# The opening of a two-layer encoder trunk: gains transposed ahead of x, x's high part taken from PSUM tile by tile, first splits in a written order, bf16 filling products

## The chip, the cores and the metric

The kernel runs on one core of one Trainium2 chip. The metric is the device time of one execution in microseconds. A profiled execution also gives a trace; its span runs from the first to the last instruction and is a little shorter than the device time. In the lines of the profile, PE is TensorE's matrix product, PEld its load of the stationary operand, DVE VectorE, ACT ScalarE, POOL GpSimd, SP the engine that issues most transfers; "L367" is line 367 of the kernel.

## What is computed

Two layers over 256 tokens of width 1024, everything in float32. The change touches the start of the first layer only: the root-mean-square norm of x and the gate and up projections of the first feed-forward block.

```python
def rmsnorm(x, g):
    y = x32 * lax.rsqrt(jnp.mean(x32 * x32, axis=-1, keepdims=True) + EPS)
    return (y * g.astype(jnp.float32)).astype(x.dtype)

def swiglu(h, w_gate, w_up, w_down):
    return (jax.nn.silu(h @ w_gate) * (h @ w_up)) @ w_down

for i in range(DEPTH):
    x = x + 0.5 * swiglu(rmsnorm(x, ffn1_norm[i]), ffn1_w_gate[i], ffn1_w_up[i], ffn1_w_down[i])
    h = rmsnorm(x, mix_norm[i])
    ...                                  # self attention and memory attention on h, projections
    x = x + jnp.concatenate([o_s, o_m], axis=-1) @ w_out[i]
    x = x + 0.5 * swiglu(rmsnorm(x, ffn2_norm[i]), ffn2_w_gate[i], ffn2_w_up[i], ffn2_w_down[i])
```

The widths: x is (256, 1024), w_gate and w_up are (1024, 2816), w_down (2816, 1024).

## The kernel before

**Products of float32 by two parts.** Each float32 operand is split into a high part of the type fp32r, which TensorE takes in one pass, and a low part, the difference. A product is then three matmuls into one PSUM bank (`dense`): high by high (line 542), high by the weight's low part (545), low of x by the weight's high part (548). Weights are split after they have landed: ScalarE copies the raw block to the high part (`split_hi`, line 367), VectorE subtracts (`split_lo`, line 385).

**The feed-forward block.** The 2816 columns go in 11 groups of 256. A chunk of weights is 512 rows of one group, gate beside up, 128 x 2048 in SBUF, in four blocks `q` of 128 rows. Three raw buffers and four pairs of split buffers rotate. For each chunk both token tiles (`tb` 0 and 1, 128 tokens each) pass through the four blocks: 24 matmuls of 128 x 512. The first four chunks are (group 0, rows 0 to 511), (group 1, rows 0 to 511), (group 0, rows 512 to 1023), (group 1, rows 512 to 1023); of the first chunk, blocks 0 and 1 are taken for both token tiles, then blocks 2 and 3.

**The opening.** The first chunk's load comes in four pieces (gate and up for each block), the second's in two, every later one in one. The order of the issues is: the first feed-forward norm's gains (`g1row`, on ScalarE's queue), the first half of x for token tile 0, block 0's gate (SP) and up (ScalarE's queue), the first half of x for tile 1, the rest of the first chunk, the second chunk, the second halves of x, the third chunk. TensorE meanwhile multiplies the identity by itself (`warm`, float32). x's halves (128 x 512) are prepared by `prep_half`: four transposes into a PSUM bank, one VectorE product with the gains into `y` (line 612), one ScalarE copy of `y` to the high part `xh` (650), one VectorE subtraction to the low part `xl` (654). The gains themselves are rows when they land: TensorE transposes them (`gps`, line 1762), VectorE copies them to `gcol` (1764). Three microseconds later on the planner's clock a ScalarE square of the half of x follows (`square`, line 667); the row norm's factor is applied only when a group's products leave PSUM (`evac`, line 728).

**What sets the order.** The program is a list of instructions per engine in the order in which Python emits them. That order comes from a model clock, `Flow`: `now` is TensorE's time, `free` holds the times at which ScalarE, VectorE and GpSimd become free; steps are generators that wake at a time or on a condition, and each emitted instruction moves the clock by an estimate (`flow.pe`, `flow.act`, `flow.dve`). `loader`, `split_hi` and `split_lo` are such generators and go by estimated arrivals (`c.block`, `c.arrive`, from `dma_free`). The hardware keeps each engine's order, and its semaphores keep the dependencies, whatever the estimates say. At the start the order is: five `warm` products, `now` set to 2.7, the gains' transpose at 3.9 with two more fillers and one at 5.6, and `prep_half` for the four halves of x at 3.4, 5.8, 12.6 and 13.4.

Of the kernel before, what the change touches and what calls it, by code (L numbers as in the profile page):

```python
# [12 lines left out]
F32 = mybir.dt.float32  # L13
# [3 lines left out]
AF = mybir.ActivationFunctionType  # L17
# [3 lines left out]
P = 128  # L21
# [20 lines left out]
T_TR = 0.107  # L42
SLACK = 0.4
AHEAD = 0


class Flow:
# [10 lines left out]
        (self.idle if idle else self.threads).append([self.now, gen])  # L58

    def pe(self, dur):  # L60
        self.now += dur
        return self.now + HOP

    def eng(self, e, dur):
# [103 lines left out]
def kernel(  # L168
# [34 lines left out]
    def bank(name, shape=(P, 4, P)):  # L203
        return banks.take(list(shape), F32, name)
# [67 lines left out]
    class Item:  # L272
# [3 lines left out]
        def __init__(self, raws, uses=8, w=1):  # L276
            self.raws, self.uses = raws, uses
            self.hi = self.lo = None
            self.hit, self.lot, self.st = [None] * 7, [None] * 7, [None] * 4
            self.n, self.frees, self.takes, self.gives, self.guest = 1, 1, 0, 0, False  # L280
            self.sums, self.t = [], []
            self.index = len(items)
            w = 1 if len(items) < 2 else w
            self.units = [(self.own(q, w), q, w, None) for q in range(0, 4, w)]
            items.append(self)

# [7 lines left out]
            return ts[q // 4][:, q % 4 * 512:(q % 4 + w) * 512]  # L294

    chunks, items = [], []
    raw_left = [NRAW]
    hl_left = [NHL]
    xt_room = [False]
# [12 lines left out]
    def loader():  # L312
        for i, c in enumerate(chunks):
            yield lambda: raw_left[0] > 0
            raw_left[0] -= 1
            c.raw = wraw.tile([P, 2048], F32, tag="raw", name=f"raw{i}")
            dma_free[0] = max(dma_free[0], flow.now)
            n = len(c.parts)
            lat = LAT + slow[0] if i > 1 else 0.6
            for j, (dst, src) in enumerate(c.parts):  # L320
                (nc.scalar if i == 0 and j == 1 else nc.sync).dma_start(out=dst(c.raw), in_=src)
                dma_free[0] += 3.0 / n
                if i < 2 and j % 2:
                    for q in range((j - 1) * 4 // n, (j + 1) * 4 // n):
                        c.block[q] = dma_free[0] + lat
                if i == 0 and j == 1:
                    table_hint(AF.Silu)
                    load_x(1, 0)
                    dma_free[0] += 0.75
            c.arrive = dma_free[0] + lat  # L330
            c.block = [t or c.arrive for t in c.block]
            if i == 1:
                for tb in range(2):
                    load_x(tb, 1)
                    dma_free[0] += 0.75
            if i > 4 and late_done[0] < len(late_loads):
                dst, src = late_loads[late_done[0]]
                late_done[0] += 1
                nc.sync.dma_start(out=dst, in_=src)
                dma_free[0] += 0.3  # L340
# [7 lines left out]
    def split_hi():  # L348
        for i, it in enumerate(items):
            yield lambda: (hl_left[0] >= it.n and all(r.raw is not None for r in it.raws)  # L350
                           and (xt_room[0] or not it.guest))
            hl_left[0] -= it.n
            if it.guest:
                xt_room[0] = False
            yield max(r.block[0] for r in it.raws)
            it.hi, it.lo = ([whl.tile([P, 2048], F32R, tag=x, name=f"{x}{i}_{j}") for j in range(it.n)]
                            for x in ("hi", "lo"))
            if it.guest:
                for x, ts in (("xh", it.hi), ("xl", it.lo)):
                    ts += [xtp.tile([P, KT, P], F32R, tag=f"{x}{j}", name=f"g{x}{j}") for j in range(2)]  # L360
            for src, q, w, dep in it.units:
                yield max(r.arrive if dep is not None else r.block[q + w - 1] for r in it.raws)
                if dep is not None:
                    yield lambda: it.st[dep] is not None
                    yield it.st[dep]
                yield calm_a(i)
                nc.scalar.copy(out=it.part(0, q, w), in_=src())  # L367
                t = flow.act(512 * w)
                it.hit[q:q + w] = [t] * w

    def split_lo():
        for i, it in enumerate(items):
            if it.sums:
                yield lambda: all(r.raw is not None for r in it.raws) and g2.left >= it.takes + 2
                yield max(r.arrive for r in it.raws)
                it.t += [g2.take([P, 512], F32, "wsum") for _ in range(it.takes)]
                for j, (x, y) in enumerate(it.sums):
                    yield calm_v(i)
                    nc.vector.tensor_sub(it.t[j], x(), y())  # L379
                    it.st[j] = flow.dve(512)  # L380
            for src, q, w, dep in it.units:
                yield lambda: it.hit[q] is not None
                yield it.hit[q]
                yield calm_v(i)
                nc.vector.tensor_sub(it.part(1, q, w), src(), it.part(0, q, w).bitcast(F32))  # L385
                t = flow.dve(512 * w)
                it.lot[q:q + w] = [t] * w
            raw_left[0] += it.frees
            g2.give(it.gives)
# [80 lines left out]

    def plan_ffn(l, nm, wg, wu, wd):
        def parts(g, c):
            pieces = (4, 2)[len(chunks)] if len(chunks) < 2 else 1
            a = cols4(wg[l], c, g * 256, 256, 0, pieces)
            b = cols4(wu[l], c, g * 256, 256, 256, pieces)
            return [q for ab in zip(a, b) for q in ab]

        gu = {}
        pair = PAIR[l, nm]
        work = [(g, c) for g in range(NG) for c in range(2)]  # L480
        if (l, nm) == (0, 1):
            work[:4] = [(g, c) for c in range(2) for g in range(2)]
        if pair is not None:
            rest = [w for w in work if w[0] not in (pair, pair + 1)]
            n = 2 * pair
            p = iter(rest[n:])
            work = rest[:n]
            loads = {}
            for x in ("11", "m1", "p", "12", "m5", "p", "22", "m7", "p", "m6", "p", "m3", "p", "p", "21", "m2", "p", "m4"):
                work.append(next(p) if x == "p" else x)  # L490
            work += list(p)
            blocks = {"11": (pair, 0), "12": (pair + 1, 0), "22": (pair + 1, 1), "21": (pair, 1)}
            raws = [Chunk(parts(*blocks[x])) for x in ("11", "12", "22", "21")]
            made, mk = pair_items(raws)
            which = dict(zip(("11", "12", "22", "21"), raws))
        for w in work:
            if w in ("11", "12", "22", "21"):
                chunks.append(which[w])
            elif isinstance(w, str):
                mk[w]()  # L500
            else:
                gu[w] = add_chunk(parts(*w), 8, 2)
        plan[l, nm, "gu"] = gu
        plan[l, nm, "work"] = [w for w in work if w not in ("11", "12", "22", "21")]
        if pair is not None:
            plan[l, nm, "pair"] = made
        dn = []
        for c in range(NG):
            dn.append(add_chunk(turned2(wd[l], c)))
            if c in SEVEN[l, nm]:  # L510
                seven_item(dn[-1], c != SEVEN[l, nm][0])
            elif c >= NG - 3:
                u = dn[-1].units
                u[1], u[2] = u[2], u[1]
        plan[l, nm, "dn"] = dn
# [1240 lines left out]
    flow.step()  # L1756
    xt = Xt(PAIR[0, 1] is not None)

    def start_gain():
        yield 3.9  # L1760
        tp = bank("gps0")
        nc.tensor.transpose(out=tp[:, 0, :16], in_=g1row, identity=ident[:16, :16])
        yield flow.pe(T_TR)
        nc.vector.tensor_copy(gcol[:, 0:16], tp[:, 0, :16])
        banks.give()
        flow.dve(16)
        first_gain.append(True)
        warm(2)
        yield 5.6
        warm(1)  # L1770

    def start(tb, hf, t):
        yield t
        yield from prep_half(xt, tb, hf, GC_FFN1, 3.0)

    def warm(n):
        for _ in range(n):
            nc.tensor.matmul(out=wb[:, 0, :], lhsT=ident, rhs=ident, start=True, stop=True)

    wb = bank("warm")  # L1780
    banks.give()
    warm(5)
    flow.now = 2.7
    flow.spawn(start_gain())
    for tb in range(2):
        for hf in range(2):
            flow.spawn(start(tb, hf, (3.4, 12.6, 5.8, 13.4)[2 * tb + hf]))
    flow.spawn(gain_columns())
    flow.spawn(rope_setup(), idle=True)
    flow.spawn(lambda_setup())  # L1790
# [59 lines left out]
```

## Time and profile before

| | us |
|---|---|
| median of 3 runs | 948.93 |
| lowest and highest | 948.30, 949.33 |
| the profiled execution | 948.83 |
| its span | 947.0 |
| first product with weights starts, from the span's start | 7.42 |
| first product of the second chunk starts | 15.06 |

The page also has the DMA's share. Slice by slice (40 slices of 23.7 us) it reads so:

```profile
DMA  9968799688525486896847679775632367589561
GB/s 296 284 212 250 228 325 329 231 268 254 178 90 164 121 258 210 266 291 225 259 143 217 214 233 290 236 252 173 203 130 76 131 219 225 188 260 329 183 217 47
```

A digit is the mean busy share of the 16 DMA engines in tenths. Records of matmuls overlap: one of 128 x 512 lasts 0.39 us in the trace while the next starts 0.23 us after it, so the pace is read from the distance of the starts. A row of the timeline joins equal instructions of one engine that follow each other ("x4"), with the start of the first and the time to the end of the last.

### The profile page before, as it was taken

Reading aid. Unit: us, or ns where it says so; the run is one execution under the profiler, and the core shown is the slowest. Engines: PE = TensorE matmul, PEld = TensorE weight load, DVE = VectorE, ACT = ScalarE, POOL = GpSimd, SP = SyncE. Lnnn points to the kernel's source line nnn. Section 1 sums busy time; section 2 is a strip of 40 time slices with the busy share of each in tenths; the row PEclk is TensorE's granted clock in tenths of the full one; section 3 lists DMA queues with packets and bytes.
Section 4 is the critical chain, followed back from the end, with each engine's and each line's share of the span. In section 5 each row is a group of like instructions: output and inputs, shape, how many; then the busy total and the mean of one; then the engine's idle time right before and its main releaser. Section 6 shows DMA issues by size and latency. Waiting matters only on the chain. (4 is left out here: it accounts for less than half of the span.)

```text
span 947.0 us, 13323 instructions
## 1 busy us (share of the span) xinstructions
PE 940.3 (99%) x4456; PEld 773.2 (82%) x4456; DVE 829.7 (88%) x1501; ACT 590.8 (62%) x1126; POOL 108.6 (11%) x160
## 2 busy tenths in 40 slices
PE   9999999999999999999999999999999999999998
PEld 7888888887878888888888888888887788888887
DVE  6989988888777889989889899796999899998995
ACT  6656666677786746647546656563777765655671
POOL 0000038731210000000000000000334100000000
PEclk9999999999999999999999999999999999999999
DMA  9968799688525486896847679775632367589561
GB/s 296 284 212 250 228 325 329 231 268 254 178 90 164 121 258 210 266 291 225 259 143 217 214 233 290 236 252 173 203 130 76 131 219 225 188 260 329 183 217 47
DMA packets 172574, 206.13 MB, mean 218 GB/s; under 512 B 10265, under 2 KB 147290, under 8 KB 172506
## 3 DMA queue, kind: packets, MB, share of 16 engines
q1 hardware_dynamic: 169498, 202.92, 67.0%
q10 hardware_dynamic: 3008, 2.37, 0.8%
q8 instruction: 35, 0.57, 0.2%
q14 instruction: 33, 0.27, 0.1%
HBM read 190.04 MB, written 15.20 MB: 217 GB/s over the span
## 5 line engine op out<-in xcount | busy, mean ns | idle before, releaser
L367 ACT CAST hi<-raw 128x512 fp32r<-128x512 f32 (+1 forms) x466 | 334.8, 770 | 152.4 <-DMA raw<-in_ffn_w_up_dram 45.7
L385 DVE TENSOR_TENSOR lo<-raw,hi 128x512 fp32r<-128x512 f32 (+1 forms) x466 | 392.2, 877 | 23.1 <-ACT hi L367 22.5
L548 PE MATMUL gu<-hi,xl 128*128 128x512 f32 x528 | 206.0, 390 | 0.0
L542 PE MATMUL gu<-hi,xh 128*128 128x512 f32 x528 | 206.0, 390 | 0.0
L545 PE MATMUL gu<-lo,xh 128*128 128x512 f32 x528 | 205.8, 390 | 0.0
L545 PEld LDWEIGHTS gu<-lo,xh 128*128 128x128 f32 x528 | 99.2, 188 | 21.0 <-DVE lo L385 0.4
L548 PEld LDWEIGHTS gu<-hi,xl 128*128 128x128 f32 x528 | 99.3, 188 | 21.0 <-DVE xl L654 0.4
L542 PEld LDWEIGHTS gu<-hi,xh 128*128 128x128 f32 x528 | 99.4, 188 | 20.4
L548 PE MATMUL acc<-hi,ht 128*128 128x512 f32 x270 | 105.6, 391 | 0.0
L542 PE MATMUL acc<-hi,ht 128*128 128x512 f32 x270 | 105.1, 389 | 0.0
L545 PE MATMUL acc<-lo,ht 128*128 128x512 f32 x270 | 105.1, 389 | 0.0
L367 ACT CAST hi<-wsum 128x512 fp32r<-128x512 f32 x83 | 49.0, 620 | 40.0 <-DVE wsum L379 37.0
L548 PE MATMUL pj<-hi,xl 128*128 128x512 f32 x160 | 63.9, 400 | 0.0
L545 PE MATMUL pj<-lo,xh 128*128 128x512 f32 x160 | 63.6, 397 | 0.0
L542 PE MATMUL pj<-hi,xh 128*128 128x512 f32 x160 | 63.5, 397 | 0.0
L545 PEld LDWEIGHTS acc<-lo,ht 128*128 128x128 f32 x270 | 50.7, 188 | 10.6
L542 PEld LDWEIGHTS acc<-hi,ht 128*128 128x128 f32 x270 | 50.7, 188 | 10.4
L548 PEld LDWEIGHTS acc<-hi,ht 128*128 128x128 f32 x270 | 50.7, 188 | 10.4
L585 POOL TENSOR_TENSOR xr<-v,nhalf 128x1 f32<-128x1 f32 x12 | 8.6, 719 | 429.6 <-DVE v L583 429.6
L385 DVE TENSOR_TENSOR lo<-wsum,hi 128x512 fp32r<-128x512 f32 x83 | 53.7, 676 | 0.0
L728 ACT ACTIVATE sil<-gu,xr 128x256 f32<-128x256 f32 x72 | 33.8, 469 | 24.7 <-PE gu L548 23.1
L585 POOL TENSOR_TENSOR hf<-v,nhalf 128x8 f32<-128x8 f32 (+1 forms) x20 | 32.1, 1607 | 83.2 <-DVE v L583 74.1
(244 smaller groups left out, 1531.5 us busy)
## 6 DMA issues: line engine op xcount, KB each, us to landing
raw<-in_ffn_w_down_dram SPq DMA_DIRECT2D x176, 256.0 KB, 4.4
raw<-in_ffn_w_gate_dram SPq DMA_DIRECT2D x82, 512.0 KB, 4.6
raw<-in_ffn_w_up_dram SPq DMA_DIRECT2D x82, 512.0 KB, 5.2
raw<-in_w_in_dram SPq DMA_DIRECT2D x32, 512.0 KB, 5.1
hd<-hb SPq DMA_DIRECT2D x44, 256.0 KB, 4.9
hr<-hd SPq DMA_DIRECT2D x44, 256.0 KB, 5.1
raw<-in_w_out_dram SPq DMA_DIRECT2D x8, 1024.0 KB, 4.9
raw<-in_w_mem_kv_dram SPq DMA_DIRECT2D x4, 1024.0 KB, 9.0
```

The source lines that it names most:

```text
L367: nc.scalar.copy(out=it.part(0, q, w), in_=src())
L385: nc.vector.tensor_sub(it.part(1, q, w), src(), it.part(0, q, w).bitcast(F32))
L542: nc.tensor.matmul(out=ps, lhsT=xh, rhs=wh, start=start, stop=False)
L545: nc.tensor.matmul(out=ps, lhsT=xh, rhs=wl, start=False, stop=False)
L548: nc.tensor.matmul(out=ps, lhsT=xl, rhs=wh, start=False, stop=stop)
L585: nc.gpsimd.tensor_tensor(out=dst, in0=v[:, :n], in1=nhalf[:, :n], op=ALU.pow)
L728: nc.scalar.activation(sil, ps[tb][:, 0:256], AF.Silu, scale=xt.r[tb])
```

## The change

It replaces the opening by a written order, and gives the planner other numbers for the first 7.5 us and the first three chunks.

- Filling products: bf16, 128 x 128, on a zeroed stretch of `junk` (a memset on VectorE), 23 at the start, two behind the gains' transpose and five behind the first four transposes of x, in place of five, two and one in float32 on the identity.
- The gains' transpose and its copy are emitted ahead of x's transposes.
- Token tile 0, first half: ScalarE takes the high part of each 128 x 128 tile from PSUM with the gain as its scale (`high`), with the weight blocks' high parts 0 and 1 in between; VectorE makes `y` from PSUM (`scaled`), then the low part of weight block 0, then x's low part.
- Token tile 1, first half: `y` as before, high part by one ScalarE copy of `y` behind block 2's high part; VectorE makes block 1's low part between `y` and the low part of x.
- The squares of x's first halves are set to 18.0 on the planner's clock. The second halves are started at 13.2 and 14.0.
- The third chunk is loaded in two pieces and split block by block. The first three chunks' arrivals are constants (`FIRST`).
- `Flow.pe` doubles each product's duration while `now` is under 7.5.

```diff
+COLD = 7.5
...
     def pe(self, dur):
-        self.now += dur
+        self.now += dur * (2 if self.now < COLD else 1)
...
-            w = 1 if len(items) < 2 else w
+            w = 1 if len(items) < 3 else w
...
+    FIRST = ((4.7, 6.1, 6.9, 8.6), (10.2, 10.2, 12.1, 12.1), (15.1, 15.1, 16.6, 16.6))
...
-                if i < 2 and j % 2:
+                if i < 3 and j % 2:
                     for q in range((j - 1) * 4 // n, (j + 1) * 4 // n):
-                        c.block[q] = dma_free[0] + lat
+                        c.block[q] = FIRST[i][q]
...
-            c.arrive = dma_free[0] + lat
+            c.arrive = dma_free[0] + lat if i > 2 else FIRST[i][3]
...
-            yield max(r.block[0] for r in it.raws)
+            if i:
+                yield max(r.block[0] for r in it.raws)
...
             for src, q, w, dep in it.units:
+                if i == 0 and q < 3:
+                    continue
...
             for src, q, w, dep in it.units:
+                if i == 0 and q < 2:
+                    continue
...
-            pieces = (4, 2)[len(chunks)] if len(chunks) < 2 else 1
+            pieces = (4, 2, 2)[len(chunks)] if len(chunks) < 3 else 1
...
-    def start_gain():
-        yield 3.9
-        tp = bank("gps0")
...
-        warm(2)
-        yield 5.6
-        warm(1)
-
-    def start(tb, hf, t):
-        yield t
-        yield from prep_half(xt, tb, hf, GC_FFN1, 3.0)
+    wz = junk[:, 0:P]
+    nc.vector.memset(wz, 0.0)
+    wb = bank("warm")
+    banks.give()
 
     def warm(n):
         for _ in range(n):
-            nc.tensor.matmul(out=wb[:, 0, :], lhsT=ident, rhs=ident, start=True, stop=True)
-
-    wb = bank("warm")
+            nc.tensor.matmul(out=wb[:, 0, :], lhsT=wz, rhs=wz, start=True, stop=True)
+
+    def turned(tb):
+        tp = bank("xtp")
+        return tp, [turn(tp[:, k, :], xs[tb][:, k * P:(k + 1) * P]) + 0.1 for k in range(4)]
+
+    def high(tb, tp, k):
+        nc.scalar.activation(xt.h[tb][:, k, :], tp[:, k, :], AF.Copy, scale=gcol[:, GC_FFN1 + k:GC_FFN1 + k + 1])
+        xt.th[tb][k] = flow.act(P)
+
+    def scaled(tb, tp):
+        y = xt.y[tb, 0] = g2.take([P, 4, P], F32, "y")
+        nc.vector.tensor_tensor(out=y, in0=tp, in1=gcol[:, GC_FFN1:GC_FFN1 + 4].unsqueeze(2).broadcast_to([P, 4, P]),
+                                op=ALU.mult)
+        banks.give()
+        return flow.dve(512)
+
+    def low(tb):
+        nc.vector.tensor_sub(xt.l[tb][:, 0:4, :], xt.y[tb, 0], xt.h[tb].bitcast(F32)[:, 0:4, :])
+        xt.t[tb][0:4] = [flow.dve(512)] * 4
+        flow.spawn(square(xt, tb, 0, 18.0))
+
+    def first_hi(q):
+        nc.scalar.copy(out=items[0].part(0, q), in_=items[0].own(q)())
+        items[0].hit[q] = flow.act(512)
+
+    def first_lo(q):
+        nc.vector.tensor_sub(items[0].part(1, q), items[0].own(q)(), items[0].part(0, q).bitcast(F32))
+        items[0].lot[q] = flow.dve(512)
+
+    def start(tb, t):
+        yield t
+        yield from prep_half(xt, tb, 1, GC_FFN1, 3.0)
+
+    warm(23)
+    tp = bank("gps0")
+    nc.tensor.transpose(out=tp[:, 0, :16], in_=g1row, identity=ident[:16, :16])
+    nc.vector.tensor_copy(gcol[:, 0:16], tp[:, 0, :16])
     banks.give()
+    warm(2)
+    first_gain.append(True)
+    flow.now = 4.0
+    tp, _ = turned(0)
     warm(5)
-    flow.now = 2.7
-    flow.spawn(start_gain())
-    for tb in range(2):
-        for hf in range(2):
-            flow.spawn(start(tb, hf, (3.4, 12.6, 5.8, 13.4)[2 * tb + hf]))
+    flow.free.update(A=4.3, V=4.95)
+    high(0, tp, 0)
+    flow.free["A"] = 4.7
+    first_hi(0)
+    for k in range(1, 4):
+        high(0, tp, k)
+    flow.free["A"] = 6.05
+    first_hi(1)
+    scaled(0, tp)
+    first_lo(0)
+    low(0)
+    flow.now = 5.35
+    tp, _ = turned(1)
+    scaled(1, tp)
+    flow.free["A"] = 6.85
+    first_hi(2)
+    nc.scalar.copy(out=xt.h[1][:, 0:4, :], in_=xt.y[1, 0])
+    xt.th[1][0:4] = [flow.act(512)] * 4
+    first_lo(1)
+    low(1)
+    for tb, t in ((0, 13.2), (1, 14.0)):
+        flow.spawn(start(tb, t))
```

More of the change, by code (lines that the diff above doesn't have):

```diff
@@ L1757 @@
     xt = Xt(PAIR[0, 1] is not None)
-    def start_gain():
-        yield 3.9
-        tp = bank("gps0")
[L1762 to L1767, printed above, removed]
-        warm(2)
-        yield 5.6
-        warm(1)
-    def start(tb, hf, t):
-        yield t
-        yield from prep_half(xt, tb, hf, GC_FFN1, 3.0)
+    wz = junk[:, 0:P]
```

## The prediction

> **What bounds the kernel now.** I read the page's busy times first, then TensorE alone in five stretches of the span, then its waits.
>
> ```profile
> PE 940.3 (99%) x4456; PEld 773.2 (82%) x4456; DVE 829.7 (88%) x1501; ACT 590.8 (62%) x1126; POOL 108.6 (11%) x160
> ```
> ```profile
> 20.00:220.00 200.00, 200.00 (x884) 1.00 0.84 269
> 220.00:320.00 100.00, 98.89 (x606) 1.00 0.46 144
> 320.00:660.00 340.00, 340.00 (x1512) 1.00 0.73 232
> 660.00:780.00 120.00, 119.62 (x658) 1.00 0.48 153
> ```
> ```profile
> PE warm L1778 <- POOL ident masks.py:199: 1.4, 1, 1.4
> PE qktp L578 <- DVE qkn L1049: 1.1, 1, 1.1
> PE xtp L578 <- DMA x<-in_x_dram: 0.2, 1, 0.2
> ```
>
> TensorE is the bound: in the feed-forward stretches (first and third row) it has one product per 200/884 = 0.226 us and 340/1512 = 0.225 us, with no gap. Only the two mixers (second and fourth row) show idle time. So whatever the opening gains before TensorE falls into that pace goes straight to the end, as long as weights, ScalarE and VectorE stay ahead, and nothing else in the change can gain. The question is how much of the opening is lost now. That is read from TensorE's timeline, and beside it that of VectorE and ScalarE:
>
> ```profile
> 1.35 2.50 PE L1778 MATMUL warm<-ident 128*128 128x128 f32 x10 [1.35 <-POOL ident masks.py:199]
> 4.01 1.11 PE L578 MATMUL xtp<-ident,x 128*128 128x128 f32 x4 [0.15 <-DMA x<-in_x_dram]
> 5.05 0.28 PE L1762 MATMUL gps<-ident,g1row 16*128 16x16 f32 x1
> 5.27 1.65 PE L1778 MATMUL warm<-ident 128*128 128x128 f32 x6
> 6.71 1.06 PE L578 MATMUL xtp<-ident,x 128*128 128x128 f32 x4
> 7.42 0.78 PE L542 MATMUL gu<-hi,xh 128*128 128x512 f32 x1
> 8.00 0.63 PE L545 MATMUL gu<-lo,xh 128*128 128x512 f32 x1
> 8.42 0.63 PE L548 MATMUL gu<-hi,xl 128*128 128x512 f32 x1
> 8.85 0.45 PE L542 MATMUL gu<-hi,xh 128*128 128x512 f32 x1
> 9.15 0.50 PE L545 MATMUL gu<-lo,xh 128*128 128x512 f32 x1
> 9.49 0.39 PE L548 MATMUL gu<-hi,xl 128*128 128x512 f32 x1
> ...
> 10.36 0.50 PE L548 MATMUL gu<-hi,xl 128*128 128x512 f32 x1
> ...
> 11.41 0.40 PE L542 MATMUL gu<-hi,xh 128*128 128x512 f32 x1
> ...
> 15.06 0.39 PE L542 MATMUL gu<-hi,xh 128*128 128x512 f32 x1
> ```
> ```profile
> 4.72 0.62 ACT L367 CAST hi<-raw 128x512 fp32r<-128x512 f32 x1 [1.57 <-DMA raw<-in_ffn_w_up_dram]
> ...
> 5.38 0.17 DVE L1764 COPY gcol<-gps 128x16 f32<-128x16 f32 x1 [5.38 <-PE gps L1762]
> ...
> 5.58 0.69 DVE L612 TENSOR_TENSOR y<-xtp,gcol 128x512 f32<-128x512 f32 x1
> ...
> 6.31 0.62 ACT L650 CAST xh<-y 128x512 fp32r<-128x512 f32 x1 [0.97 <-DVE y L612]
> ...
> 6.83 1.13 ACT L367 CAST hi<-raw 128x512 fp32r<-128x512 f32 x2
> ...
> 7.81 0.69 DVE L612 TENSOR_TENSOR y<-xtp,gcol 128x512 f32<-128x512 f32 x1 [0.15 <-PE xtp L578]
> ...
> 8.42 1.28 DVE L385 TENSOR_TENSOR lo<-raw,hi 128x512 fp32r<-128x512 f32 x2
> ...
> 9.62 0.69 DVE L654 TENSOR_TENSOR xl<-y,xh 128x512 fp32r<-128x512 f32 x1
> ```
>
> The first real product starts at 7.42. The next ones stand 0.43 apart (8.00, 8.42, 8.85), from 9.49 on 0.23: TensorE ran at half pace until about 9.1, though the clock column says 1.00 throughout. The fifth product (9.15) waited for the second weight block's low part (8.42 + 0.68 = 9.10), the ninth (10.36) for the low part of x's second token tile (9.62 + 0.69 = 10.31). The thirteenth, at 11.41, is the first of 12 that wait for nothing: 12 x 0.23 + 8 transposes x 0.11 = 3.6, and the next chunk begins at 15.06. So **the place to compare is the thirteenth product**. It is late because VectorE's chain is late: the gains' column at 5.38 (gps stands behind x's four transposes on TensorE), y at 5.58, and the second y only at 7.81, since x's second tile is transposed behind three fp32 filling products that run until 6.7.
>
> **The change part by part.**
>
> Filling products: five plus three fp32 ones go, 30 in bf16 on zeros come (23, 2 and 5); each fp32 one is two records, 2.50/10 = 0.25 us a record. They no longer wait for the identity at 1.35 but for a memset on VectorE, idle before 5.38; I take a start at 1.0. Bf16 on 128 columns isn't in the trace; the nearest is the attention's one-pass product at full pace:
>
> ```profile
> 756.51 1.09 PE L1571 MATMUL AV<-PT,vm 128*64 128x128 f32 x16
> 757.54 0.50 PE L542 MATMUL acc<-hi,oT 128*128 128x512 f32 x1
> ```
>
> (757.54 - 756.51)/16 = 0.064, at half pace 0.13. Bounds: nothing, and 0.25 as an fp32 record. By 0.13 the 23 end at 1.0 + 23 x 0.13 = 4.0; by 0.25 at 6.75, 2.7 later than x's tile needs TensorE. With gps (0.28) and two more fillers (0.26) in front, x's transposes then begin at 4.0 to 4.5 instead of 4.01. The Trainium skill, "TensorE: Matmul & The Clock Gate", Part 1, has 0.107 us for such a product in the cold state: by it the 23 end at 3.5 and the transposes begin at 4.01 as now. No row here shows it.
>
> Gains' transpose ahead of x: gps and the gcol copy (0.28 and 0.17) are done before the first x tile's record ends (4.48 at the earliest). What is queued behind it on TensorE is everything, so a late g1row would delay all; it is issued at the same time as x's first half, and 8 KB against 256. Taken as no wait.
>
> x's high part tile by tile: ScalarE scales four 128x128 tiles out of PSUM instead of one 128x512 copy of y (0.62). The nearest row:
>
> ```profile
> L1603 ACT ACTIVATE pe<-S,nm 128x128 f32<-128x128 f32 x12 | 4.3, 368 | 1.5 <-DVE nm L1596 1.0 <-DVE S L1593 0.5
> ```
>
> Four at 0.37 are 1.5 us, 0.9 more of ScalarE, hidden: first tile 4.5 to 4.9, weight block 0's high part 4.8 to 5.4, other tiles to 6.3, block 1 to 6.9 and block 2 to 7.5 (both had landed when they ran at 6.83 without a wait).
>
> VectorE's chain, with rows of now (0.61 from start to start): y 5.17 to 5.86 (last transpose ends at 5.12), low part of block 0 until 6.47, xl until 7.08. The second tile's landing:
>
> ```profile
> DMA to landing us min/median/max: 3.2/4.4/5.6
> ```
>
> Issued at 1.65, it is in at 4.9 to 6.0. Its transposes follow the five fillers at about 5.6 and end by 6.7, so the second y runs 7.01 to 7.70 (now 7.81), block 1's low part until 8.30 (now 9.10), xl, after a ScalarE copy 7.75 to 8.37, until 9.10 (now 10.31).
>
> TensorE then: first product 6.45, at half pace 7.0, 7.45, 7.87, the fifth at 8.35, then 8.78 and the seventh at 9.2, from where the pace is full if the clock changes when it does now; 6 x 0.225 more put the thirteenth at 10.53 instead of 11.41: 0.88 saved. With transposes at 4.45 everything is 0.35 to 0.44 later, 0.5 saved. I take **0.7**, the middle, both ends being equally near a row.
>
> The clock decides the rest. If full pace came before 6.4, the fifth product still waits until 8.35 and the thirteenth starts at 10.2: 1.2 saved. It could also come later: now it comes 3.8 us after the filling that begins at 5.27 and runs on without a gap; if the wait before the fifth product starts that count anew at 8.35, it comes at 12.15, 2.95 us more run at half pace and 2.95 x (1 - 0.226/0.43) = 1.4 are lost: 0.7 slower than now. The row that bears on it: fed from 1.35 with one short gap at 3.9, TensorE was still at half pace at 8.85, 7.5 us on. The same page, Part 1, says full clock comes after one busy window of 3.4 us, windows running freely, so at the latest 6.8 us after the start; the trace disagrees by 0.7 us unless the gap or the transposes spoil a window, and Part 4 says that transposes don't count as busy. By the first rule the new filling would bring full pace by 7.8, by the second the window from 5.6 to 9 (four transposes, a wait before the fifth product) may fail; both ends are above.
>
> Edits at no cost: the third chunk comes in two pieces and is split by 512 columns. VectorE has four of 0.69 for two of 1.23, 0.3 more, ScalarE about as much; SP issues four loads for two, 0.9 more, the x halves already being past it.
>
> ```profile
> 17.56 2.36 DVE L385 TENSOR_TENSOR lo<-raw,hi 128x1024 fp32r<-128x1024 f32 x2 [0.46 <-ACT hi L367]
> ...
> 23.50 0.47 ACT L728 ACTIVATE sil<-gu,xr 128x256 f32<-128x256 f32 x1
> ```
>
> That split is done at 19.9; TensorE wants the chunk at 15.06 + 24 x 0.226 = 20.5, its second half at 21.9, with the change 0.7 earlier: cover of over 1 us, and the halves land earlier. The first halves' squares move to 18, four of 0.8 in a row, and are wanted by the gate's activation, now 23.50. If that cover went, only ScalarE would wait: each group keeps two of eight PSUM banks.
>
> **The sum**: 948.83 (the profiled execution; its span 947.0 plus 1.8 around it) - 0.7 = 948.1; beside the median of 948.93, **948.2**, own range 947.5 to 948.9.
>
> **The rivals.**
>
> The planner's order. The list of instructions is written by a model clock, which now starts elsewhere and doubles the cost of products until 7.5. The feed-forward stretches have nothing to lose by it, the mixers do; there the chain leaves TensorE:
>
> ```profile
> 736.16 2.30 issue
> 738.46 0.47 ACT junk L1635 x2
> ...
> 742.17 0.86 PE S L1487 x9
> ```
>
> Better: that 2.30 goes, 948.2 - 2.3 = 945.9. Worse, the other side: another such 2.3 and another wait of 1.1 as for qktp, 951.6. It decides if a mixer step moves by over one product, 0.23. Against both: the decisions hang on the plan's own TensorE time, which a shift moves together.
>
> The clock comes late: 948.93 + 0.7 = 949.6. For it, the wait before the fifth product; against it, the fillers now run with hardly a gap from 1.0.
>
> The change doesn't do what it says: fillers at over 0.15, or a late g1row, give back the 0.7: 948.9.
>
> **How the numbers follow.** Forecast 0.55; better order 0.20; late clock 0.10; nothing gained 0.08; worse order 0.07. About 0.2% (1.9 us) is what a measurement of this kernel tells from no change. Faster by over that: the better order and a little of the forecast's edge, 0.23; slower: the worse order and the fillers' upper bound, 0.08; within: 0.69. The range 945.9 to 950.3 takes in the better order and the late clock with half a microsecond; it leaves out the worse order and the fillers' dearest end.
>
> **What would show it.** gcol before 4.5; the first product near 6.45, not 7.42; the fifth near 8.35 and the ninth without a wait for xl; the thirteenth 0.5 to 1.2 before 11.41; the first product of the second chunk as much before 15.06; TensorE's idle time in the mixers as now. A difference that is absent at 15 us and there at 330 or 780 would be the planner's; products 0.43 apart after 9.5 would be the clock's.

## The result and the profile after

| | before | after |
|---|---|---|
| median, us (5 runs each, on one chip) | 948.73 (948.30 to 949.33) | 957.91 (956.03 to 959.51) |
| ratio, 95% interval | | 1.0093 [1.0082, 1.0105] |
| the profiled execution, its span, us | 948.83, 947.0 | 957.33, 955.5 |

The change made the kernel 9.2 us slower; 948.2 was forecast, and the range ended at 950.3. TensorE is as much the bound as it was: the first part of the page of after, the busy times, has

```profile
PE 945.3 (99%) x4470; PEld 773.1 (81%) x4470; DVE 828.4 (87%) x1504; ACT 591.7 (62%) x1131; POOL 106.8 (11%) x160
```

The same engine is busy for 5 us more with the same products but for the filling. Cut into the stretches of the prediction (us, TensorE's busy time and products, granted clock, DMA share, GB/s), after reads

```profile
20.00:220.00 200.00, 198.70 (x865) 1.00 0.79 256
220.00:320.00 100.00, 98.04 (x592) 0.98 0.52 167
320.00:660.00 340.00, 340.00 (x1511) 1.00 0.72 232
```

The second feed-forward block of the layer (third row) is as it was, 1511 products against 1512. The first has 865 where before had 884: 19 x 0.226 = 4.3 us. The mixer has 592 where before had 606, and a clock below 1. So there are three places: the opening, the first feed-forward stretch and the first mixer. TensorE's timeline shows the first:

```profile
0.98 2.63 PE L1773 MATMUL warm<-junk 128*128 128x128 bf16 x23 [0.98 <-DVE junk L1767]
3.64 0.25 PE L1809 MATMUL gps<-ident,g1row 16*128 16x16 f32 x1
...
4.01 1.06 PE L585 MATMUL xtp<-ident,x 128*128 128x128 f32 x4
...
6.04 0.49 PE L549 MATMUL gu<-hi,xh 128*128 128x512 f32 x1
8.15 0.50 PE L552 MATMUL gu<-lo,xh 128*128 128x512 f32 x1 [1.62 <-DVE lo L1800]
...
10.97 0.63 PE L549 MATMUL gu<-hi,xh 128*128 128x512 f32 x1
11.39 0.63 PE L552 MATMUL gu<-lo,xh 128*128 128x512 f32 x1
...
12.90 0.39 PE L549 MATMUL gu<-hi,xh 128*128 128x512 f32 x1
```

The filling, the gains and x's transposes come as forecast or earlier, and the first product at 6.04 instead of 7.42. The second then waits 1.62 us for the low part of weight block 0; the third (8.75) and the fifth (9.95) wait for low parts again, with 0.6 from one product to the next; from 10.5 to 12 products stand 0.43 apart, which is half pace; and the thirteenth starts at 12.90, 1.5 later than before (11.41) and 2.4 later than forecast. What VectorE did meanwhile stands in its timeline, beside ScalarE's:

```profile
5.11 0.37 ACT L1780 ACTIVATE xh<-xtp,gcol 128x128 fp32r<-128x128 f32 x1 [1.97 <-PE xtp L585]
5.38 0.61 ACT L1796 CAST hi<-raw 128x512 fp32r<-128x512 f32 x1
5.89 0.89 ACT L1780 ACTIVATE xh<-xtp,gcol 128x128 fp32r<-128x128 f32 x3
...
3.93 0.17 DVE L1810 COPY gcol<-gps 128x16 f32<-128x16 f32 x1 [3.00 <-PE gps L1809]
6.80 0.69 DVE L1785 TENSOR_TENSOR y<-xtp,gcol 128x512 f32<-128x512 f32 x1 [2.70 <-ACT xh L1780]
7.41 0.68 DVE L1800 TENSOR_TENSOR lo<-raw,hi 128x512 fp32r<-128x512 f32 x1
```

VectorE's y waits until 6.80, and not for TensorE, whose transposes were done by 5.11, but for ScalarE: its last three tiles end at 6.78. Both engines read the same PSUM bank, `xtp`; they only read it, yet the program makes the one wait for the other. Four tiles with a weight block between them thus hold VectorE for 1.7 us.

The second place needs the window from 60 to 140. Before and after:

```profile
60.00:140.00 80.00, 80.00 (x354) 1.00 0.82 261
```
```profile
60.00:140.00 80.00, 78.70 (x337) 1.00 0.76 243
```

17 products fewer are 3.8 us. Compared product by product (the start of a product in after less that of the same product in before, at its time in before), after is 1.5 us late from 16 to 72, 5.4 at 126, 5.5 at 214, 8.2 at 330 and 8.4 at the end. The list of TensorE's waits names the last engine in the chain, VectorE, but shows little of it, as short waits aren't listed:

```profile
PE qktp L585 <- DVE qkn L1056: 2.0, 1, 2.0
...
PE gu L552 <- DVE lo L392: 1.1, 2, 0.9
```

### The profile page after: what moved, and what is told of

The parts are those of the page before. It is cut to its first block, busy times and chain, and to the rows that moved or that the text cites. A ratio compares the mean times of both kernels' runs of the same rounds, so it can differ in the third digit from the quotient of the medians.

```text
span 955.5 us, 13352 instructions
## 1 busy us (share of the span) xinstructions
PE 945.3 (99%) x4470; PEld 773.1 (81%) x4470; DVE 828.4 (87%) x1504; ACT 591.7 (62%) x1131; POOL 106.8 (11%) x160
## 5 line engine op out<-in xcount | busy, mean ns | idle before, releaser
L738 DVE SCALAR_TENSOR_TENSOR h<-gu,xr,sil 128x256 f32<-128x256 f32 x72 | 34.3, 476 | 11.8 <-ACT sil L735 11.8
```

Source lines behind the costliest of these rows:

```text
L738: nc.vector.scalar_tensor_tensor(out=h, in0=ps[tb][:, 256:512], scalar=xt.r[tb], in1=sil, op0=ALU.mult, op1=ALU.mult)
```

## The experiments

Below, "opening" means what TensorE, ScalarE and VectorE do until about 9 us, "order" the order of the engines' lists behind it, which the plan writes, and "hour" a time on the plan's own clock. Of the plan, two numbers are tried: the hour of the squares of x's first halves (18.0 in after; in before 3 us behind each half's preparation, about 10 and 12.5), and the plan's hour at which the second chunk begins (14.257 in before, 12.723 in after).

**The shared bank.** In e1 ScalarE makes x's first high part with one copy of y, as before; the order behind it is that of after, instruction by instruction (the traces of both have the same 1504 instructions of VectorE in the same order).

```diff
-        nc.scalar.activation(xt.h[tb][:, k, :], tp[:, k, :], AF.Copy, scale=gcol[...])
         xt.th[tb][k] = flow.act(P)
...
+    scaled(0, tp)
+    nc.scalar.copy(out=xt.h[0][:, 0:4, :], in_=xt.y[0, 0])
     flow.free["A"] = 6.05
     first_hi(1)
-    scaled(0, tp)
```

> The changed kernel, but x's first high part is made by one ScalarE copy of y behind VectorE's product, as before the change; every other instruction stands in the changed order on every engine. Theory bank: VectorE's y waited for ScalarE's four reads of the same PSUM bank (6.80); here y starts at 5.1 to 5.2, and the opening is 0.5 to 1.2 ahead of the kernel before. Theory lateness (VectorE's two microseconds lost at the opening are what stops TensorE later, at 74 to 125 and in the first mixer): no loss behind the opening, 947.5 to 949.5 in all. Rival, theory order (the planner's other order of the rest costs it, whatever the opening does): the opening gains, and 5 to 7 are lost behind it all the same, 953 to 955.

Measured: 955.32 us, ratio to before 1.0065 [1.0044, 1.0086]. The five executions go from 953.03 to 958.07, and the traced one is the fastest, so its timelines show less loss than the median has; the same holds for e4, e5 and e6. The timelines of e1, VectorE and then TensorE:

```profile
5.08 0.69 DVE L1784 TENSOR_TENSOR y<-xtp,gcol 128x512 f32<-128x512 f32 x1 [1.00 <-PE xtp L585]
...
8.40 0.50 PE L552 MATMUL gu<-lo,xh 128*128 128x512 f32 x1 [0.47 <-DVE lo L1799]
...
10.35 0.39 PE L549 MATMUL gu<-hi,xh 128*128 128x512 f32 x1
```

y now follows the transposes, and the opening is the forecast one: the fifth product at 8.40 (8.35), the thirteenth at 10.35 (10.53). Product by product e1 is 1.1 us ahead of before from 16 to 90, 2.3 behind by 126 and 4.1 at the end: the opening's gain is real, and a loss of its own lies behind it.

e2 keeps ScalarE's four tiles and takes the reason of the wait away: x's four tiles are transposed twice, into a bank that ScalarE reads (`xtq`) and one that VectorE reads.

```diff
+    tq = bank("xtq")
+    banks.give()
+    for k in range(4):
+        nc.tensor.transpose(out=tq[:, k, :], in_=xs[0][:, k * P:(k + 1) * P], identity=ident)
     tp, _ = turned(0)
...
-        high(0, tp, k)
+        high(0, tq, k)
```

> The changed kernel with x's first four tiles transposed twice, into a bank that ScalarE alone reads and one that VectorE alone reads; the rest of every engine's order is the changed one. Theory bank: VectorE's y starts when the second set of transposes ends, at 5.9 to 6.1, while ScalarE still reads its tiles, and no wait for ScalarE stands before it; if the wait had another cause, y stays at 6.8 or later. Theory lateness: about half of the loss goes, 949 to 953. Theory order: 1 less than the changed kernel at most, 955.5 to 957.5.

Measured: 956.55 us, 1.0077 [1.0059, 1.0095]. VectorE's timeline in e2:

```profile
5.79 0.69 DVE L1785 TENSOR_TENSOR y<-xtp,gcol 128x512 f32<-128x512 f32 x1 [1.62 <-PE xtp L585]
```

y waits for the (second) transposes alone and runs from 5.79 to 6.48, while ScalarE's last three tiles run from 5.95 to 6.83. So it was the bank, and not VectorE's need of anything that ScalarE makes. The Trainium skill, "PSUM — Partial Sum Buffer", section "PSUM bank collisions raise a hardware error", says that two engines may not access one bank and group of 32 partitions at once, ScalarE's reads against VectorE's included, and that the compiler's scheduler therefore puts a dependency between them. The traces agree as far as they go: with one bank the second reader stood still until the first had ended, with two it didn't.

**A late opening by itself.** e3 is before with three copies of x on VectorE, into a stretch that nobody reads, behind the gains' column: VectorE's chain is late as in after (the three copies take 1.34 us, and y starts at 6.59), and the order is that of before.

```diff
         nc.vector.tensor_copy(gcol[:, 0:16], tp[:, 0, :16])
         banks.give()
+        for _ in range(3):
+            nc.vector.tensor_copy(junk, xs[0][:, 0:512])
```

> The kernel before with three extra VectorE copies of x into junk (0.6 each, 1.8 in all) behind the gains' copy, which the planner is not told of: the order of the kernel before on every engine, VectorE 1.8 late at the opening. Theory lateness: TensorE loses 1 to 3 at the opening (the wait and half pace after it) and more at 74 to 125 and in the first mixer, 953 to 958 in all. Theory order: the opening's loss alone, 950 to 951.8, and TensorE has no wait for a weight's low part behind 20 us.

Measured: 949.82 us, 1.0010 [1.0001, 1.0019]. What the copies cost in the opening reaches the end, about 1 us, and nothing is lost later.

**Opening against order.** e4 has the opening of before, and behind it the plan's numbers of after with the order that they make; e5 the opening of after, and the plan's two hours put back:

```diff
             for ks in ((0, 1), (2, 3)):
                 plain_chunk(0, 0, range(2), ks)
+            flow.at(14.257)
             work = work[1:]
...
-        flow.spawn(square(xt, tb, 0, 18.0))
+        flow.spawn(square(xt, tb, 0, (10.0, 12.5)[tb]))
```

and e4, beside the planner's numbers of the change's diff (`COLD`, `FIRST`, the third chunk in two pieces), has in before:

```diff
-            flow.spawn(square(xt, tb, hf, flow.now + wait))
+            flow.spawn(square(xt, tb, hf, 18.0 if hf == 0 else flow.now + wait))
...
+            flow.now = 12.723
...
-            flow.spawn(start(tb, hf, (3.4, 12.6, 5.8, 13.4)[2 * tb + hf]))
+            flow.spawn(start(tb, hf, (3.4, 13.2, 5.8, 14.0)[2 * tb + hf]))
```

> The opening of the kernel before (fp32 filling, x's transposes ahead of the gains', high part from y), but the planner is given the changed kernel's numbers: third chunk in two pieces, squares of the first halves at 18.0, second halves of x at 13.2 and 14.0, and its clock set to 12.72 (the changed kernel's hour) when the second chunk begins. From there on the order on TensorE is the changed kernel's, and on the other engines but for a dozen neighbours exchanged before 75 us. Theory order: TensorE's first 20 us as in the kernel before, then waits for low parts at 72 to 125 and in the first mixer, 952 to 957. Rival, theory opening (what the opening does to the engines is what costs): 948.3 to 949.8.

> The reverse: the changed kernel's opening unaltered, with VectorE's wait for ScalarE's four reads and the clock as it comes, but the squares of the first halves go back to 10.0 and 12.5 on the planner's clock, which then waits until 14.26 (the hour of the kernel before) at the end of the first chunk. From the second chunk's splits on the order is that of the kernel before. Theory order: what the opening costs alone, 0.9 to 1.9 more than before: 949.6 to 950.8. Theory opening: 955 to 959.

Measured: e4 958.65 us, 1.0098 [1.0083, 1.0113]; e5 950.85, 1.0019 [1.0010, 1.0028]. The opening of before with the new order is as slow as after; the new opening with the old order loses 1.9 to 2.1 us. Order, not lateness, carries the main loss. e6 puts the mends together, e1's copy and e5's two hours:

> The opening of e1 (high part by one copy of y) with the order of the kernel before from the second chunk on, as in e5. Theory order: the second chunk begins 1.0 to 1.6 earlier than in the kernel before and nothing is lost behind it: 946.9 to 947.9, faster than both. Theory opening has no reason for a loss here either: 947 to 949; the run tells whether the opening's gain reaches the end.

Measured: 948.24 us, 0.9992 [0.9983, 1.0001].

**Which hour?** e7 is before with the squares of the first halves at 18.0, and nothing else. e10 is e1 with the squares alone put back, e11 e1 with the hour of the second chunk alone put back, and e12 is after with the squares alone put back.

```diff
-        flow.spawn(square(xt, tb, 0, 18.0))
+        flow.spawn(square(xt, tb, 0, (10.0, 12.5)[tb]))
```

> The kernel before with one edit to the planner: the squares of x's first halves at 18.0 on its clock instead of 3 behind their low parts. This is the single input of the plan that moves most other decisions (some 170 rows of VectorE's order against the kernel before). Theory order, as chance arrangement: a loss somewhere between nothing and that of e4, 949 to 955; if the squares alone carry it, that of e4. Theory opening: 948.5 to 949.2.

> The changed kernel with x's first high part by one copy of y, and the squares of the first halves of x back at 10.0 and 12.5; the plan's hour of the second chunk stays that of the changed order. Theory squares (four squares in a row on ScalarE hold the high parts, the low parts, the raw buffers and so the loads): 948 to 950.5 us, loads at 36 us at most 3 later than before. Theory hour (the plan's earlier hour at the second chunk puts the pair's sums ahead of the low parts): 952 to 956 us, loads 6 to 7 late at 36 us as before this edit.

> The changed kernel with x's first high part by one copy of y, and the plan's hour at the second chunk set to 14.257 as the kernel before has it; the squares stay at 18.0. Theory squares: 951 to 956 us, loads still 1.4 us late from 23 us on and TensorE losing time in the mixer. Theory hour: 948 to 950 us, loads at 36 us at most 3 late.

> The changed kernel with one edit: the squares of the first halves of x back at 10.0 and 12.5 in the plan; x's high part stays tile by tile out of PSUM. Theory squares (the squares' hour carries the loss of the order, the shared bank only the opening's): the opening's loss stays, the rest goes, 950.5 to 951.5 us, loads at 36 us 2 to 4 late. Theory both together (the later opening upsets the order by itself): 953 to 958 us, loads at 36 us 7 or more late.

| | opening | squares | us | ratio to before |
|---|---|---|---|---|
| e7 | before | 18.0 | 951.52 | 1.0029 [1.0017, 1.0041] |
| e11 | e1 | 18.0 | 955.11 | 1.0065 [1.0044, 1.0085] |
| e1 | e1 | 18.0 | 955.32 | 1.0065 [1.0044, 1.0086] |
| e10 | e1 | 10.0, 12.5 | 948.96 | 0.9999 [0.9989, 1.0009] |
| after | after | 18.0 | 957.91 | 1.0093 [1.0082, 1.0105] |
| e12 | after | 10.0, 12.5 | 950.86 | 1.0024 [1.0014, 1.0034] |

In the new plan it is the squares' hour: that one number takes 7.05 us off after (e12) and 6.4 off e1 (e10); the second chunk's hour takes nothing off e1 that can be measured (e11). In the plan of before the same number costs 2.5 (e7). How can the place of four ScalarE instructions that nobody waited for in before cost so much? The traces show two ways. The first is the queue behind them. ScalarE and VectorE at that place, first in after, then VectorE in e12 and in before:

```profile
20.82 0.63 ACT L674 ACTIVATE junk<-x 128x512 bf16<-128x512 f32 x1
...
23.71 1.98 ACT L372 CAST hi<-raw 128x1024 fp32r<-128x1024 f32 x2
...
23.08 0.16 DVE L683 TENSOR_TENSOR sst<-xss 128x1 f32<-128x1 f32 x1 [1.04 <-ACT junk L674]
...
24.77 2.36 DVE L392 TENSOR_TENSOR lo<-raw,hi 128x1024 fp32r<-128x1024 f32 x2 [0.59 <-ACT hi L372]
```
```profile
20.80 2.42 DVE L392 TENSOR_TENSOR lo<-raw,hi 128x512 fp32r<-128x512 f32 x3
```
```profile
19.84 0.15 DVE L676 TENSOR_TENSOR sst<-xss 128x1 f32<-128x1 f32 x1
...
20.57 1.23 DVE L385 TENSOR_TENSOR lo<-raw,hi 128x1024 fp32r<-128x1024 f32 x1 [0.39 <-ACT hi L367]
```

The two squares that were moved now stand with those of the second halves: four in a row hold ScalarE from 20.82 to 23.71. VectorE, which adds up what they sum (`sst`), now waits for them, 1.04 us and once more 0.41; in before no such wait stands. Behind them on ScalarE stands the high part of the fourth chunk, behind that, on VectorE, its low part, at 24.77, 4.2 us later than in before. In e12 it is the last of the three that the row joins, 1.22 long, and starts at 22.00, 1.4 later than in before. With the low part the raw buffer becomes free into which SP's next load goes. In before, and with the hours put back, the squares stand one by one between the high parts.

Between e1 and e10 the queue explains nothing, though e1's four squares stand in a row too, from 18.25 to 21.14, and e10 differs from it by the squares' hour alone. VectorE and SP in e1, and then in e10:

```profile
22.21 2.36 DVE L392 TENSOR_TENSOR lo<-raw,hi 128x1024 fp32r<-128x1024 f32 x2 [0.59 <-ACT hi L372]
...
35.54 2.85 DVE L887 TENSOR_TENSOR y<-y 128x512 f32<-128x512 f32 x4
...
43.26 0.33 SPq L323 DMA_DIRECT2D raw<-in_ffn_w_gate_dram  x1
```
```profile
22.03 1.23 DVE L392 TENSOR_TENSOR lo<-raw,hi 128x1024 fp32r<-128x1024 f32 x1 [1.59 <-ACT hi L372]
...
37.26 2.86 DVE L887 TENSOR_TENSOR y<-y 128x512 f32<-128x512 f32 x4
...
38.37 0.41 SPq L323 DMA_DIRECT2D raw<-in_ffn_w_gate_dram  x1
```

The fourth chunk's low part starts at 22.21 and 22.03, the load ahead of the one shown at 36.11 and 36.41; the next is 4.9 us later in e1. So the second way is the plan: the squares move its clock for ScalarE, and it lists what follows otherwise (about 150 of VectorE's 1504 instructions stand in another order in e1 than in e10). One such place is the first row of sums of the feed-forward pair (`y<-y` on VectorE, four of 0.69). It frees no raw buffer, and in the new order comes ahead of low parts that would free a buffer. After, VectorE and SP's queue:

```profile
38.06 2.86 DVE L887 TENSOR_TENSOR y<-y 128x512 f32<-128x512 f32 x4
...
44.50 1.22 DVE L392 TENSOR_TENSOR lo<-raw,hi 128x1024 fp32r<-128x1024 f32 x1
...
38.62 0.56 SPq L323 DMA_DIRECT2D raw<-in_ffn_w_up_dram  x1
45.78 0.33 SPq L323 DMA_DIRECT2D raw<-in_ffn_w_gate_dram  x1
```

For 7 us no weight is called for; the load at 45.78 follows the low part that ends at 45.72. How many low parts come first can be counted in VectorE's timeline (in blocks of 128 x 512 that start ahead of these sums); beside it how much later the load starts that before issues at 36.3, by position:

| low parts ahead of the pair's sums | kernels and lateness of the load, us |
|---|---|
| 32 | e6 0.3, e5 0.8, e9 1.2, e3 1.6, e10 2.0, e12 2.5 (before 0) |
| 30 | e7 4.3, e11 4.5 |
| 28 | e1 6.9, e8 7.0, e2 7.4, e4 8.7, after 9.4 |

The lateness of the load goes with the count, whichever opening a kernel has. Of the 7.0 us by which the load of after is later than that of e12, 1.4 were there at the load before it, from the queue behind the squares; 5.5 come at the sums. This is read from the traces: no run moves these sums alone. TensorE does not feel it yet: it lives on the lead of the split weights, and falls short from 72 on in after and from 90 on in e1. A second place of the kind stands there; in after, VectorE's sums of the next pair and SP's queue:

```profile
85.14 0.68 DVE L901 TENSOR_TENSOR gu_v<-gu_u,pair_m 128x512 f32<-128x512 f32 x1
...
88.18 1.21 DVE L392 TENSOR_TENSOR lo<-raw,hi 128x1024 fp32r<-128x1024 f32 x1
...
84.54 0.50 SPq L323 DMA_DIRECT2D raw<-in_ffn_w_up_dram  x1
...
89.45 0.35 SPq L323 DMA_DIRECT2D raw<-in_ffn_w_gate_dram  x1
```

e8 is e1 with those sums held until the third low part of chunk 16 is listed:

```diff
             yield g2.has(3)
+            if (l, nm) == (0, 1):
+                yield lambda: items[16].lot[2] is not None
```

> e1 (mended opening, changed order) with one step held: the pair's four VectorE sums at about 77 wait in the plan until the low part of the block ahead, whose raw buffer the next loads need, has been emitted. 18 rows of VectorE's order differ from e1, all between 76 and 130, none of TensorE's. Theory freed buffer (the sums stand ahead of that low part, so the buffer is freed 3 to 4 late, SP issues no load for over 4, and the weights are late from 90 on): the gap in the loads goes to under 2, the 3.4 that e1 lost between 90 and 125 fall to under 1.5, in all 2 to 3 less than e1: 951.5 to 954. Rival (VectorE simply has too much to do there, whatever its order): as e1, 953 to 958. Neither touches the first mixer's loss of about 3.

Measured: 954.30 us, 1.0053 [1.0038, 1.0069], just above the range that was expected if these sums were the cause; the interval overlaps that of e1. The gap of the loads shrinks from 4.0 us in e1 to 0.9, and what e1 lost from 95 to 126 (2.2 us) is gone, but from 72 to 95 3.1 are lost where e1 lost 1.2, and in the mixer 3.1 where e1 lost 1.8. So to hold these sums mends nothing that can be measured, which fits a lead that was lost before them.

**The mixer.** e7 loses nothing in the feed-forward stretch (its loads are level again at 60) and 2.8 us of the profiled execution in the first mixer (product by product it is 0.4 ahead of before at 200 and 2.4 behind at 330). VectorE and TensorE there in e7:

```profile
220.53 2.50 DVE L385 TENSOR_TENSOR lo<-raw,hi 128x512 fp32r<-128x512 f32 x4
222.94 0.75 DVE L1049 SCALAR_TENSOR_TENSOR qkn<-pj,xr,hf 128x512 f32<-128x512 f32 x1
...
223.75 0.69 PE L578 MATMUL qktp<-flip,qkn 128*128 128x128 f32 x2 [2.83 <-DVE qkn L1049]
```

The normed q and k stand behind four low parts on VectorE (three in before), and TensorE waits 2.83 us for them (1.1 in before, 2.0 in after), then runs about 3 us at half pace. The order that a plan writes at 18 us thus still decides one at 220.

**A version that keeps the gain.** e9 is e6 with eight more filling products behind x's second transposes, against the half pace of the opening:

```diff
+    warm(8)
```

> e6 with eight more filling products between the second tile's transposes and the first product, where TensorE waits for x's high part. Theory clock (e6's scatter of 947.5 to 949.8 comes from openings in which the idle stretch keeps half pace): 947.4 to 948.0 with less scatter, 0.3 to 0.7 under e6. Rival (the idle stretch is too short to matter, or the fillers delay the first product): 947.9 to 948.7, as e6.

Measured: 947.94 us, 0.9991 [0.9982, 0.9999]. It can't be told from e6; both are about 0.1% faster than before, at the edge of what the intervals tell. What their openings win (product by product 0.9 at 16 in both) is still there at the end of the profiled execution, 1.0 in e9 and 1.5 in e6.

## Why the prediction was wrong

The sum first. Forecast 948.2, measured 957.9. e12 to after is the squares' hour, 7.05; e10 to e12 the shared bank with what it draws after it, 1.90; forecast to e10 another 0.76, which lies within e10's interval (0.9 us to each side). e10's traced execution is 0.5 us ahead of before from 16 to 660 and loses this in the second mixer, with a wait of 0.4 for `m`. e6 has the plan's hour put back too and is 0.72 faster, but the intervals of the two overlap.

- **Filling and gains: right.** The filling products are 2.63/23 = 0.114 us each, between the two bounds (nothing and 0.25). That is nearer to the 0.107 of the Trainium skill ("TensorE: Matmul & The Clock Gate", Part 1) than to the 0.13 taken. The gains' column is done at 4.10, before the limit of 4.5.
- **"x's high part tile by tile": wrong.** ScalarE's 0.9 more was called hidden, and y set at 5.17. y came at 6.80, since a tile-wise reader keeps the bank from the other reader until its last tile. The step looked at ScalarE's time and at TensorE's, and not at who else reads that bank; the rule of the Trainium skill quoted with e2 speaks against just this edit and was not weighed. With it, the forecast's own tiles, done at 6.3, put y at 6.3 and the end of block 0's low part at 7.6; the tiles ended at 6.78, and the second product started at 8.15.
- **The rest of the opening: right.** e1 has the forecast y (5.08), fifth product (8.40) and thirteenth (10.35, between the 10.2 of an early clock and 10.53). But the row of before from which 0.7 was taken is itself slow: there half pace lasted until 8.96, in e4 and e7, with the same opening, until 6.07 and 4.98, and both are 0.4 ahead of before at 16.
- **The late clock (0.10): it came on top.** Half pace lasted until 12.1, where the rival had set it (12.15), behind the wait that it named as its reason, though for another product and after a stretch at full pace (from 5.29), so that the hour agrees by luck. In e5, with the same opening, it did not come in the traced execution, which is level with before at 16.
- **"Edits at no cost", the squares at 18: the step that failed.** They were put at nothing and cost 7.05 us. "If that cover went, only ScalarE would wait" is not so: VectorE waited too, 1.04 and 0.41 us. And it left out two things: what is queued behind the squares (the high part, on VectorE the low part, the raw buffer, SP's load), which made the loads of after 1.4 us later than those of e12, and that the plan, whose clock the squares move, lists what follows otherwise (28 low parts ahead of the pair's sums, not 32), which made the load at 45.78 another 5.5 later.
- **"The decisions hang on the plan's own TensorE time, which a shift moves together": wrong.** This was the reason for giving the worse order a chance of 0.07 only. The squares' hour is a number of its own and did not move with the rest; with it alone put back, the order loses little (e10, e12).
- **"The feed-forward stretches have nothing to lose by it, the mixers do": half wrong.** The mixers lost as the worse-order rival said (the wait for q and k grew by 0.9, and half pace came with it, 2.7 from 214 to 330). The first feed-forward stretch lost more, 3.9 us between 72 and 126, though TensorE had no gap there before: having no gap is no measure of the lead that keeps it so. The times at which the loads are issued show it: 9.4 us late at 36, and still 8.8 at 81.
- The rival had the right sign at 0.07, and its price of 3.4 us was too low by two thirds. The test it came with served: the difference was 1.5 at 16 and 8.2 at 330, so both the opening and the plan.

**What stays open:** why the same hour of the squares costs 2.5 to 2.8 us in the plan of before and 6.4 to 7 in the new one. It isn't the opening as it runs: e4 has that of before, as e7 has, and the squares at 18.0, as e7 has, and is 7.1 us slower. The other numbers of the new plan make the difference, and which of them (the third chunk in two pieces, the arrivals, the starts of the second halves) was not tried; the second chunk's hour alone changed nothing in e1 (e11), and without the late squares all of them cost nothing that can be measured (e10 against e6). e7 has 30 low parts ahead of the sums and e1 28, and e11, with 30, is as slow as e1; so the count explains the late loads and not all of the loss. No run keeps the squares at 18.0 and only puts these first sums behind the low parts; that they are the place is argued from the traces.

## What to carry to other kernels

An instruction that nobody waits for is free only if nothing behind it in its queue is wanted, and if the plan that lists the rest is not moved by it: before one is moved, follow the queue behind it over the next engines to the buffer that they free and the load that waits for it, and see whether an engine in that chain has slack. Where a plan writes the order, a change of its early numbers is to be tried apart from the change that it is made for, with the old numbers put back. Two engines that read one PSUM bank take turns: tile by tile by the one is late for the other, by the whole of the series (1.7 us here).

## What the runs showed of the hardware

The granted clock can fall again after a wait of about half a window. Windows of 3.4 us, of after in the opening and in the mixer (length, TensorE's busy time, clock), and then of e5:

```profile
5.30:8.70 3.40, 1.66 (x9) 1.00 0.97 293
8.70:12.10 3.40, 3.35 (x7) 0.50 1.03 342
227.20:230.50 3.30, 1.34 (x9) 1.00 0.76 230
230.60:233.90 3.30, 3.30 (x9) 0.50 0.78 242
```
```profile
4.20:7.50 3.30, 1.65 (x14) 1.00 0.92 292
7.50:10.90 3.40, 2.61 (x9) 1.00 1.01 310
```

After a window in which TensorE was busy for 1.66 of 3.4 us follows one at half pace, although TensorE is busy through it; 1.65 of 3.3, with the wait of 1.6 us across the edge of a window, was enough in e5. So a window about half busy can go either way; whether the small difference in the share or the place of the wait decides, these rows don't tell. The same opening lost 1.5 us by it in after (at 16) and nothing in e5. The Trainium skill, "TensorE: Matmul & The Clock Gate", Part 1, gives half clock after an idle window of about 3.4 us, windows running freely; the length and the freely running windows agree with these rows, but the fall came here after windows that were half busy.
